# Split weights in rings: eight tiles of 512 columns, or four of 1024

## The chip, the cores and the metric

The kernel runs on one core of one Trainium2 chip. The metric is the device time of one execution in microseconds (us), lower is better. TensorE (PE) multiplies, VectorE (DVE) and ScalarE (ACT) work element by element, GpSimd (POOL) does the same for a few small steps, and SyncE (SP) issues the transfers. Each engine runs its own instructions in the order in which they stand in its queue.

## The reference

Two layers (DEPTH 2) run over one sequence of 512 tokens with 1024 features, all in float32. In each layer the normalised input is multiplied by w_in, three groups of heads mix the tokens (differential attention, latent attention, windowed attention), and their outputs are joined by w_out. A cross-attention into 256 memory tokens follows, then a gated feed-forward of width 2816. Each of the three adds its normalised result to the stream.

```python
for l in range(DEPTH):
    h = rmsnorm(x, g_mix_pre[l])
    # three groups of heads from h @ w_in[l]: o_a, o_b, o_c
    mix = jnp.concatenate([o_a, o_b, o_c], axis=-1) @ w_out[l]
    x = x + rmsnorm(mix, g_mix_post[l])
    xo = cross_attention(rmsnorm(x, g_x_pre[l]), rmsnorm(mem, g_x_mem[l]), w_xq[l], w_xkv[l], w_xo[l])
    x = x + rmsnorm(xo, g_x_post[l])
    gate, up = jnp.split(rmsnorm(x, g_ffn_pre[l]) @ w_ffn_in[l], 2, axis=-1)
    x = x + rmsnorm((jax.nn.silu(gate) * up) @ w_ffn_out[l], g_ffn_post[l])
```

## The kernel before

**A product in three.** Every float32 operand of a large product is kept as a high part and a low part, both in the type float32r. `split` makes them: ScalarE casts the source to the high tile (L103), and VectorE subtracts that from the source to get the low tile (L104). `mm3` then issues three matmuls for each block of 128 rows: high by high (L150), and two that take one low part (L151 and L152). Which of the two takes the low weight depends on the side on which the weights stand.

**The rings.** Weights come in by `stage`, which issues the loads of one block of up to 8 x 256 columns into one of two buffers st. `unit` cuts such a block into tiles and splits each: the high tile is named wh, the low tile wl, and both come from the pool w (bufs=8 before), so that each name has a ring of eight buffers of 512 columns. A new tile waits until the matmuls of the tile that had its buffer are through. A unit whose product is a chunk of 128 output features by all tokens (`ws_chunk`) is 8 blocks of 128 columns, so two tiles before; a unit of rows of 512 columns is one tile for each row block. The last down weights of each feed-forward (`down_weights(NG - 1, True)`) also live in this ring, as four pieces of 512 columns; the other down weights have buffers of their own (dwh, dwl) and are split by operations of 1024 columns.

**The stages.** In each layer the mixing runs first (scores, softmax and values of the heads, with the projections filled in between), then the output projection (`out_late`, `out_rest`), then cross-attention (`x_attn`), its output projection, and the feed-forward (`ffn`). Between stages the four token tiles i = 0 to 3 are normalised one after the other: the post-norm squares (L202, ScalarE, one for each half), takes a root on GpSimd (L206, L207: rpost), multiplies by the gain (L236) and adds to x (L238); the pre-norm squares x, takes a root (rpre) and scales (L223 on VectorE, or L220 and L221), and `to_T` transposes the result on PE (L183) and splits it into the high and low tiles of the next stage (hx in cross-attention, hf in the feed-forward, hT in the next layer). The first products of the next stage are made for token tiles 0 and 1 first, and for 2 and 3 when these are there.

**The feed-forward.** Each of 11 groups has four units (gate and up, for two chunks), 4 x 24 matmuls, and then the eight down blocks of the group before (six matmuls each, PSUM tile ps_sc, two buffers), which VectorE adds to the accumulators (L1250; the first group is copied on ScalarE, L1248). The activation is L1233 (ScalarE) and L1234 (VectorE), and its product is split into f.

**What sets the order.** The program names the operations in the order of its code, and a scheduler then places them into the queues of the engines by priorities, dependencies and its own estimates; it does so anew when the operations change. `Head` of the next layer makes the latent projection of the next mixing while the last blocks of the feed-forward run.

## Time and profile before

| | us |
|---|---|
| median of 3 runs | 1578.89 |
| lowest and highest | 1577.57 and 1579.68 |
| the profiled execution's own time | 1577.31 |
| span of the profiled execution | 1575.5 |
| PE busy | 1538.4 |
| DVE busy | 982.5 |
| ACT busy | 804.8 |

The profile shows one execution. Its span runs from the first to the last instruction; its own time is 1.8 us longer. In rows of the time line the first number is the start, the second the duration of one instruction or of a run of equal ones (xcount), and what stands in brackets is how long the engine had been idle and what ended that.

### The profile page before, as it was taken

What the parts mean: (1) busy time and instruction counts of PE and PEld (TensorE: products, weight loads), DVE (VectorE), ACT (ScalarE), POOL (GpSimd) and SP (SyncE); (2) the same over time, 40 slices, a digit from 0 to 9 for tenths busy, and PEclk for the clock granted to TensorE, in tenths of its full rate; (3) what the DMA queues carried; (4) which work ended last, traced back from release to release, by engine and by line L of the source; (5) the groups of instructions that cost most, each with busy time, mean ns of one, the idle gap of its engine ahead of it and who ended that gap; (6) DMA issues with size and microseconds to landing.
All of it is one profiled execution on the core that took longest, in us unless ns stands there. A gap on an engine that the chain in (4) does not pass through costs nothing.

```text
span 1575.5 us, 21925 instructions
## 1 busy us (share of the span) xinstructions
PE 1538.4 (98%) x8225; PEld 1309.8 (83%) x8225; DVE 982.5 (62%) x1919; ACT 804.8 (51%) x1749; POOL 110.3 (7%) x204
## 2 busy tenths in 40 slices
PE   6999999999999999999999999999999999999998
PEld 6987987899888888888888878778888888888886
DVE  6899886765653444454566998858646444445544
ACT  4588888544643232222456788975445532322321
POOL 2200000200300000000130000002004000000000
PEclk9999999999999999999999999999999999999999
DMA  5542651241243222232335144522402423233221
GB/s 179 158 97 88 207 170 41 71 161 54 81 134 113 101 90 98 84 120 91 96 120 146 51 138 164 167 62 86 155 31 97 134 81 107 80 108 107 80 81 54
DMA packets 130298, 168.68 MB, mean 107 GB/s; under 512 B 21776, under 2 KB 100752, under 8 KB 129424
## 3 DMA queue, kind: packets, MB, share of 16 engines
q1 hardware_dynamic: 130192, 167.28, 33.1%
q8 instruction: 65, 1.06, 0.3%
q14 instruction: 41, 0.34, 0.1%
HBM read 150.88 MB, written 10.09 MB: 102 GB/s over the span
## 4 chain that ended last, share of the span: by engine, by line
PE 86%; DVE 5%; ACT 3%; POOL 3%; issue 2%; DMA 1%; SPq 0%; POOLq 0%; DVEq 0%; ACTq 0%
PE ps_mm L152 14%; PE ps_mm L151 13%; PE ps_mm L150 13%; PE ps_av L151 6%; PE ps_av L152 6%; PE ps_av L150 6%; PE ps_sc L152 5%; PE ps_sc L151 5%; PE ps_sc L150 5%; PE ps_at L416 3%; PE ps_sc L801 1%; PE ps_av L589 1%; PE ps_av L590 1%; PE ps_sc L638 1%; DVE x L238 1%
## 5 line engine op out<-in xcount | busy, mean ns | idle before, releaser
L104 DVE TENSOR_TENSOR wl<-st,wh 128x512 fp32r<-128x512 f32 (+1 forms) x406 | 275.5, 691 | 239.9 <-ACT wh L103 239.1
L103 ACT CAST wh<-st 128x512 fp32r<-128x512 f32 (+1 forms) x406 | 243.0, 616 | 294.1 <-PE ps_mm L151 125.0
L151 PE MATMUL ps_mm<-hfl,wh 128*128 128x512 f32 (+1 forms) x384 | 143.0, 372 | 1.5 <-DVE hfl L104 1.5
L152 PE MATMUL ps_av<-hfh,wl 128*128 128x512 f32 (+1 forms) x384 | 142.8, 372 | 1.3 <-DVE wl L104 1.3
L152 PE MATMUL ps_mm<-hfh,wl 128*128 128x512 f32 (+1 forms) x384 | 142.7, 372 | 1.1 <-DVE wl L104 1.1
L150 PE MATMUL ps_mm<-hfh,wh 128*128 128x512 f32 (+1 forms) x384 | 142.7, 372 | 0.6 <-ACT hfh L103 0.6
L150 PE MATMUL ps_av<-hfh,wh 128*128 128x512 f32 (+1 forms) x384 | 142.6, 372 | 0.0
L151 PE MATMUL ps_av<-hfl,wh 128*128 128x512 f32 (+1 forms) x384 | 142.6, 371 | 0.0
L150 PE MATMUL ps_sc<-dwh,f 128*128 128x512 f32 x320 | 124.7, 390 | 0.0
L151 PE MATMUL ps_sc<-dwl,f 128*128 128x512 f32 x320 | 124.5, 389 | 0.0
L152 PE MATMUL ps_sc<-dwh,f 128*128 128x512 f32 x320 | 124.5, 389 | 0.0
L103 ACT CAST dwh<-st 128x1024 fp32r<-128x1024 f32 x40 | 40.1, 1049 | 157.4 <-PE ps_sc L152 153.3
L104 DVE TENSOR_TENSOR pl<-ps_at,ph 128x512 fp32r<-128x512 f32 (+1 forms) x128 | 82.7, 654 | 22.2 <-ACT ph L103 21.0
L206 POOL TENSOR_SCALAR rpost<-rpostss 128x1 f32<-128x1 f32 x24 | 10.5, 436 | 1171.7 <-ACT hTh L202 703.4
L151 PEld LDWEIGHTS ps_mm<-hfl,wh 128*128 128x128 f32 x384 | 72.3, 188 | 15.0 <-DVE hfl L104 2.6
L152 PEld LDWEIGHTS ps_av<-hfh,wl 128*128 128x128 f32 x384 | 72.2, 188 | 14.1 <-DVE wl L104 1.7
L152 PEld LDWEIGHTS ps_mm<-hfh,wl 128*128 128x128 f32 x384 | 72.4, 189 | 13.8 <-DVE wl L104 1.3
L150 PEld LDWEIGHTS ps_mm<-hfh,wh 128*128 128x128 f32 x384 | 72.2, 188 | 13.5 <-ACT hfh L103 1.1
L150 PEld LDWEIGHTS ps_av<-hfh,wh 128*128 128x128 f32 x384 | 72.4, 188 | 12.5
L151 PEld LDWEIGHTS ps_av<-hfl,wh 128*128 128x128 f32 x384 | 72.3, 188 | 12.4
L103 ACT CAST ph<-ps_at 128x512 fp32r<-128x512 f32 (+1 forms) x128 | 70.4, 562 | 23.6 <-PE ps_at L416 22.7
L416 PE MATMUL ps_at<-ident,e 128*128 128x128 f32 x480 | 77.0, 275 | 3.8 <-DVE memTl L104 2.1
(363 smaller groups left out, 3867.2 us busy)
## 6 DMA issues: line engine op xcount, KB each, us to landing
st<-in_w_ffn_in SPq DMA_DIRECT2D x44, 1024.0 KB, 4.9
st<-in_w_ffn_out SPq DMA_DIRECT2D x22, 1024.0 KB, 4.8
st<-in_w_xkv SPq DMA_DIRECT2D x16, 1024.0 KB, 5.3
st<-in_w_out SPq DMA_DIRECT2D x16, 512.0 KB, 4.9
st<-in_w_xq SPq DMA_DIRECT2D x8, 1024.0 KB, 5.1
st<-in_w_xo SPq DMA_DIRECT2D x8, 1024.0 KB, 5.0
st<-in_w_in SPq DMA_DIRECT2D x12, 512.0 KB, 3.9
q<-stg SPq DMA_DIRECT2D x48, 128.0 KB, 2.3
```

The lines of the kernel that those rows point to most:

```text
L103: cast = nc.scalar.copy(hi, src)
L104: nc.vector.tensor_tensor(out=lo, in0=src, in1=hi.bitcast(F32), op=ALU.subtract)
L150: nc.tensor.matmul(ps, lhsT=lh, rhs=rh, start=first, stop=False)
L151: nc.tensor.matmul(ps, lhsT=lh, rhs=rl, start=False, stop=False)
L152: nc.tensor.matmul(ps, lhsT=ll, rhs=rh, start=False, stop=last)
L206: nc.gpsimd.tensor_scalar(out=r, in0=ms[:, 0:1], scalar1=ms[:, 1:2], scalar2=EPS, op0=ALU.add, op1=ALU.add)
L238: nc.vector.scalar_tensor_tensor(out=xt[i][:, sl], in0=t, scalar=r, in1=xt[i][:, sl], op0=ALU.mult, op1=ALU.add)
L416: nc.tensor.transpose(pt[:, c * P:(c + 1) * P], e[:, k * P:(k + 1) * P], ident)
L589: nc.tensor.matmul(av, lhsT=v, rhs=hi, start=k == u["k0"], stop=False)
L590: nc.tensor.matmul(av, lhsT=v, rhs=lo, start=False, stop=k == u["k1"] - 1)
L638: nc.tensor.matmul(ps, lhsT=t[:, m, 0, i * P:(i + 1) * P], rhs=t[:, m, 1, :], start=True, stop=True)
L801: nc.tensor.matmul(ps, lhsT=mla["qT"][:, h, i * P:(i + 1) * P], rhs=mla["kT"][:, h, :], start=True, stop=True)
```

## The change

The pool of the ring has four buffers instead of eight, and a tile holds up to 1024 columns instead of 512. A unit of 8 x 128 columns is then one tile, split by one cast and one subtraction of twice the width; a unit of four rows of 512 columns is two tiles. The memory of the rings stays the same. A piece of 512 columns takes a whole buffer all the same, so the last down weights fill four buffers of four, where they filled four of eight. No matmul is added or taken away.

```diff
-    wp = ctx.enter_context(tc.tile_pool(name="w", bufs=8))
+    wp = ctx.enter_context(tc.tile_pool(name="w", bufs=4))
...
         a, b = st_view.shape[1], st_view.shape[2]
-        per = 512 // b
+        per = 1024 // b
```

Since the instructions changed, the scheduler's order did too. Three places are shown. Names carry buffer numbers where rows would read alike.

In a steady group of the feed-forward, VectorE's queue at the end of the fourth unit (e is the gated product, f its split, faccM the accumulator) stood like this before:

```order
L1234 TENSOR_TENSOR e<-e,ps_av 128x512
L104 TENSOR_TENSOR wl<-st,wh 128x512
L1250 TENSOR_TENSOR faccM<-faccM,ps_sc 128x512
L104 TENSOR_TENSOR f_6284<-e,f_6284 128x512
L1250 TENSOR_TENSOR faccM<-faccM,ps_sc 128x512 x3
L1250 TENSOR_TENSOR faccSq<-faccSq,ps_sc 128x512 x4
```

and stands like this now:

```order
L1234 TENSOR_TENSOR e<-e,ps_av 128x512
L104 TENSOR_TENSOR wl<-st,wh 128x1024
L104 TENSOR_TENSOR f_5369<-e,f_5369 128x512
L1250 TENSOR_TENSOR faccM<-faccM,ps_sc 128x512 x4
L1250 TENSOR_TENSOR faccSq<-faccSq,ps_sc 128x512 x4
```

The last low split is the wide one, and f stands ahead of the first accumulation instead of behind it.

On PE at the same place, the down blocks (ps_sc, six matmuls each) and the first unit of the next group (ps_mm) before, from the third block on:

```order
L150 MATMUL ps_sc_6899<-dwh_6877,f0_6505 128x512
L151 MATMUL ps_sc_6899<-dwl_6878,f0_6505 128x512
L152 MATMUL ps_sc_6899<-dwh_6877,f0_6505 128x512
L150 MATMUL ps_sc_6899<-dwh_6877,f0_6505 128x512
L151 MATMUL ps_sc_6899<-dwl_6878,f0_6505 128x512
L152 MATMUL ps_sc_6899<-dwh_6877,f0_6505 128x512
```

and now, from the end of the second block on:

```order
L150 MATMUL ps_sc_6543<-dwh_6529,f0_6189 128x512
L151 MATMUL ps_sc_6543<-dwl_6530,f0_6189 128x512
L152 MATMUL ps_sc_6543<-dwh_6529,f0_6189 128x512
L150 MATMUL ps_mm_6612<-hfh0_4533,wh_6604 128x512
L151 MATMUL ps_mm_6612<-hfl0_4534,wh_6604 128x512
L152 MATMUL ps_mm_6612<-hfh0_4533,wl_6605 128x512
L150 MATMUL ps_mm_6612<-hfh0_4533,wh_6604 128x512
L150 MATMUL ps_sc_6551<-dwh_6529,f0_6189 128x512
L151 MATMUL ps_sc_6551<-dwl_6530,f0_6189 128x512
L152 MATMUL ps_sc_6551<-dwh_6529,f0_6189 128x512
```

Four matmuls of the next group's first unit stand between the second and the third block; before they came behind the eighth.

At the start of cross-attention, VectorE's queue around the normalisation of token tile 3 (x3, scaled into the tiles c), with the low tiles of units 1 to 3 and the transposed tiles hxl, before (the low tiles of unit 1 had come earlier):

```order
L236 TENSOR_TENSOR e_3893<-ps_av_3605,gains_3685 128x512
L238 SCALAR_TENSOR_TENSOR x3_3695<-e_3892,rpost_3889,x3_3695 128x512
L238 SCALAR_TENSOR_TENSOR x3_3695<-e_3893,rpost_3889,x3_3695 128x512
L104 TENSOR_TENSOR wl_3923<-st_3920,wh_3922 128x512
L104 TENSOR_TENSOR wl_3927<-st_3920,wh_3926 128x512
L223 SCALAR_TENSOR_TENSOR c_3904<-x3_3695,rpre_3901,gains_3685 128x512
L104 TENSOR_TENSOR hxl0_3689<-ps_at_3966,hxh0_3688 128x4x128
L104 TENSOR_TENSOR hxl1_3691<-ps_at_3973,hxh1_3690 128x4x128
L223 SCALAR_TENSOR_TENSOR c_3905<-x3_3695,rpre_3901,gains_3685 128x512
L104 TENSOR_TENSOR wl_3931<-st_3920,wh_3930 128x512
L104 TENSOR_TENSOR wl_3935<-st_3920,wh_3934 128x512
```

and now:

```order
L236 TENSOR_TENSOR e_3733<-ps_av_3445,gains_3525 128x512
L238 SCALAR_TENSOR_TENSOR x3_3535<-e_3732,rpost_3729,x3_3535 128x512
L238 SCALAR_TENSOR_TENSOR x3_3535<-e_3733,rpost_3729,x3_3535 128x512
L104 TENSOR_TENSOR wl_3753<-st_3412,wh_3752 128x1024
L104 TENSOR_TENSOR hxl0_3529<-ps_at_3794,hxh0_3528 128x4x128
L104 TENSOR_TENSOR hxl1_3531<-ps_at_3801,hxh1_3530 128x4x128
L223 SCALAR_TENSOR_TENSOR c_3744<-x3_3535,rpre_3741,gains_3525 128x512
L223 SCALAR_TENSOR_TENSOR c_3745<-x3_3535,rpre_3741,gains_3525 128x512
L104 TENSOR_TENSOR wl_3759<-st_3756,wh_3758 128x1024
L104 TENSOR_TENSOR wl_3763<-st_3756,wh_3762 128x1024
```

The low tile of unit 1 stands behind the residual of tile 3 (L238), and those of units 2 and 3 behind both scalings of c. On PE the products of unit 1 (ps_av) followed the transposes of o before:

```order
L183 MATMUL ps_at_3973<-ident_95,o_3845 128x128 x4
L150 MATMUL ps_av_3939<-hxh0_3688,wh_3912 128x256
L151 MATMUL ps_av_3939<-hxl0_3689,wh_3912 128x256
L152 MATMUL ps_av_3939<-hxh0_3688,wl_3913 128x256
L150 MATMUL ps_av_3939<-hxh0_3688,wh_3912 128x256
L151 MATMUL ps_av_3939<-hxl0_3689,wh_3912 128x256
L152 MATMUL ps_av_3939<-hxh0_3688,wl_3913 128x256
```

and now units 2 and 3 begin ahead of the first product with a low tile:

```order
L183 MATMUL ps_at_3801<-ident_95,o_3685 128x128 x4
L150 MATMUL ps_av_3767<-hxh0_3528,wh_3752 128x256
L151 MATMUL ps_av_3767<-hxl0_3529,wh_3752 128x256
L150 MATMUL ps_mm_3768<-hxh0_3528,wh_3758 128x256
L151 MATMUL ps_mm_3768<-hxl0_3529,wh_3758 128x256
L150 MATMUL ps_av_3769<-hxh0_3528,wh_3762 128x256
L151 MATMUL ps_av_3769<-hxl0_3529,wh_3762 128x256
L152 MATMUL ps_av_3767<-hxh0_3528,wl_3753 128x256
L150 MATMUL ps_av_3767<-hxh0_3528,wh_3752 128x256
```

Two matmuls each of units 1, 2 and 3 stand ahead of the L152 that reads the low tile.

At the start of the feed-forward in layer 1, VectorE's queue around the normalisation of token tiles 2 and 3 (scaled into o and c), with the transposed tiles hfl and the low tiles of units 0 to 3, before:

```order
L223 SCALAR_TENSOR_TENSOR o_5050<-x2_3694,rpre_5054,gains_4718 128x512
L104 TENSOR_TENSOR wl_5141<-st_5130,wh_5140 128x512
L104 TENSOR_TENSOR wl_5145<-st_5130,wh_5144 128x512
L236 TENSOR_TENSOR e_5106<-ps_mm_5060,gains_4718 128x512
L238 SCALAR_TENSOR_TENSOR x3_3695<-e_5105,rpost_5102,x3_3695 128x512
L238 SCALAR_TENSOR_TENSOR x3_3695<-e_5106,rpost_5102,x3_3695 128x512
L104 TENSOR_TENSOR wl_5213<-st_5128,wh_5212 128x512
L104 TENSOR_TENSOR wl_5217<-st_5128,wh_5216 128x512
L223 SCALAR_TENSOR_TENSOR c_5112<-x3_3695,rpre_5116,gains_4718 128x512
L104 TENSOR_TENSOR hfl0_4722<-ps_at_5174,hfh0_4721 128x4x128
L104 TENSOR_TENSOR hfl1_4724<-ps_at_5181,hfh1_4723 128x4x128
L104 TENSOR_TENSOR wl_5221<-st_5130,wh_5220 128x512
```

and now:

```order
L223 SCALAR_TENSOR_TENSOR o_4830<-x2_3534,rpre_4834,gains_4530 128x512
L104 TENSOR_TENSOR wl_4917<-st_4910,wh_4916 128x1024
L104 TENSOR_TENSOR wl_4985<-st_4908,wh_4984 128x1024
L236 TENSOR_TENSOR e_4886<-ps_mm_4840,gains_4530 128x512
L238 SCALAR_TENSOR_TENSOR x3_3535<-e_4885,rpost_4882,x3_3535 128x512
L238 SCALAR_TENSOR_TENSOR x3_3535<-e_4886,rpost_4882,x3_3535 128x512
L104 TENSOR_TENSOR hfl0_4534<-ps_at_4946,hfh0_4533 128x4x128
L104 TENSOR_TENSOR hfl1_4536<-ps_at_4953,hfh1_4535 128x4x128
L104 TENSOR_TENSOR wl_4989<-st_4910,wh_4988 128x1024
L223 SCALAR_TENSOR_TENSOR c_4892<-x3_3535,rpre_4896,gains_4530 128x512
```

The split of unit 2 moved ahead of the residual of tile 3 (L238), and that of unit 3 ahead of the scaling of c (L223).

## Rows read from the trace of the kernel before

**Rows 1.** Busy times and shares of all engines, the page's first part.

```profile
PE 1538.4 (98%) x8225; PEld 1309.8 (83%) x8225; DVE 982.5 (62%) x1919; ACT 804.8 (51%) x1749; POOL 110.3 (7%) x204
```

**Rows 2.** Windows: length, busy time (instructions) per engine, PEclk, DMA share, GB/s.

```profile
80.00:120.00 40.00, 39.89 (x214) 33.44 (x213) 38.68 (x97) 32.21 (x72) 0.00 (x0) 1.00 0.38 92
...
480.00:740.00 260.00, 260.00 (x1148) 215.35 (x1148) 121.88 (x170) 77.13 (x118) 0.00 (x0) 1.00 0.29 96
```

**Rows 3.** Windows of tile wl alone: PE, PEld, DVE.

```profile
80.00:120.00 40.00, 14.70 (x38) 6.96 (x37) 6.73 (x10) 1.00 0.38 92
```

**Rows 4.** Groups by form: busy, mean ns of one, idle before.

```profile
L104 DVE TENSOR_TENSOR wl<-st,wh 128x512 fp32r<-128x512 f32 x386 | 264.4, 697 | 238.7 <-ACT wh L103 238.0
...
L104 DVE TENSOR_TENSOR dwl<-st,dwh 128x1024 fp32r<-128x1024 f32 x40 | 47.2, 1222 | 32.7 <-ACT dwh L103 32.7
...
L103 ACT CAST wh<-st 128x512 fp32r<-128x512 f32 x386 | 232.5, 620 | 288.5 <-PE ps_mm L151 120.4 <-PE ps_av L151 103.0 <-DMA st<-in_w_ffn_in 37.4
...
L103 ACT CAST dwh<-st 128x1024 fp32r<-128x1024 f32 x40 | 40.1, 1049 | 157.4 <-PE ps_sc L152 153.3 <-DMA st<-in_w_ffn_out 4.1
```

**Rows 5.** Time line of DVE: start, us, equal operations in a run.

```profile
280.61 2.50 DVE L104 TENSOR_TENSOR wl<-st,wh 128x512 fp32r<-128x512 f32 x4 [0.54 <-ACT wh L103]
...
520.58 2.36 DVE L104 TENSOR_TENSOR dwl<-st,dwh 128x1024 fp32r<-128x1024 f32 x2 [0.44 <-ACT dwh L103]
```

**Rows 6.** Time lines of PE, DVE and ACT, one group of the feed-forward.

```profile
541.01 0.39 PE L150 MATMUL ps_sc<-dwh,f 128*128 128x512 f32 x1
...
543.73 0.39 PE L150 MATMUL ps_sc<-dwh,f 128*128 128x512 f32 x1
...
542.57 0.69 DVE L1250 TENSOR_TENSOR faccM<-faccM,ps_sc 128x512 f32<-128x512 f32 x1
...
541.04 0.62 ACT L103 CAST wh<-st 128x512 fp32r<-128x512 f32 x1 [2.10 <-PE ps_av L151]
```

**Rows 7.** Time lines of PE and ACT, start of the feed-forward in both layers.

```profile
438.01 0.39 PE L152 MATMUL ps_av<-hfh,wl 128*128 128x256 f32 x1 [0.49 <-DVE wl L104]
...
1210.98 0.39 PE L152 MATMUL ps_mm<-hfh,wl 128*128 128x256 f32 x1 [1.14 <-DVE wl L104]
...
1214.89 0.39 PE L152 MATMUL ps_av<-hfh,wl 128*128 128x256 f32 x1 [0.79 <-DVE wl L104]
...
428.08 1.12 ACT L103 CAST wh<-st 128x512 fp32r<-128x512 f32 x2
```

**Rows 8.** Time lines of PE, DVE and ACT, start of cross-attention, layer 1.

```profile
309.44 1.04 PE L183 MATMUL ps_at<-ident,o 128*128 128x128 f32 x8
...
320.27 0.39 PE L151 MATMUL ps_mm<-hxl,q 128*128 128x256 f32 x1 [0.17 <-DVE hxl L104]
...
309.94 1.40 DVE L238 SCALAR_TENSOR_TENSOR x<-e,rpost,x 128x512 f32<-128x512 f32 x2
...
311.27 1.28 DVE L104 TENSOR_TENSOR wl<-st,wh 128x512 fp32r<-128x512 f32 x2
...
313.39 0.75 DVE L223 SCALAR_TENSOR_TENSOR c<-x,rpre,gains 128x512 f32<-128x512 f32 x1 [0.85 <-POOL rpre L207]
...
312.07 1.05 ACT L103 CAST hxh<-ps_at 128x512 fp32r<-128x512 f32 x2
```

**Rows 9.** Time lines of PE, ACT and DVE, start of layer 2.

```profile
790.54 0.36 PE L150 MATMUL ps_av<-wh,hTh 128*128 128x256 f32 x1
...
797.72 1.16 PE L183 MATMUL ps_at<-ident,o 128*128 128x128 f32 x8 [1.31 <-DVE hTl L104]
...
809.47 1.09 PE L183 MATMUL ps_at<-ident,c 128*128 128x128 f32 x8 [1.08 <-ACT c L221]
...
791.07 0.60 ACT L103 CAST wh<-st 128x512 fp32r<-128x512 f32 x1
...
793.57 0.68 DVE L1250 TENSOR_TENSOR faccSq<-faccSq,ps_sc 128x512 f32<-128x512 f32 x1
```

**Rows 10.** Time line of SP, the store of the distances.

```profile
54.07 0.53 SPq L334 DMA_DIRECT2D dist_dram<-dist  x1
```

## The prediction

> **What bounds the kernel now.** I read the page's busy times first [rows 1]: TensorE (PE) is busy for 1538.4 of 1575.5 us, so all of its idle time is 37 us, and a change that adds or removes no matmul moves the time only through those 37 us and through new waits. The second view is the table by windows [rows 2]: in the feed-forward stretch PE is never idle while VectorE (DVE) is busy for 121.88 of 260 us; in the mixing stretch DVE is busy for 38.68 of 40 us and PE for 39.89. So DVE has room everywhere except in mixing. The third view is the groups by form [rows 4], which price a split; the last are the rows around the places where the order of the work moves [rows 6 to 10]. PE waits for a low tile (wl) three times in all, for 0.49, 1.14 and 0.79 us [rows 7]. That is everything a cheaper split could give back directly.
>
> **What the change removes.** 193 pairs of splits of 512 columns become 193 of 1024 (386 of the old form on each engine [rows 4]; the 416s and 384s go the same way). Mean durations say 2 x 0.697 - 1.222 = 0.172 us saved on DVE for each pair. Back to back it is less: four low splits take 2.50 us, so they start (2.50 - 0.69) / 3 = 0.603 us apart, and two of 1024 start 2.36 - 1.22 = 1.14 us apart [rows 5]; a pair saves 2 x 0.603 - 1.14 = 0.066 us. A queue that runs dry saves nothing. Only mixing has a full DVE queue: ten low splits lie in its first window [rows 3], so about 40 in its four windows (two in each layer), an estimate; 20 pairs x 0.066 = 1.3 us of DVE time. PE is idle for only 0.11 us in that window, so I take half: **-0.6 us**. Bounds: -3.4 (20 x 0.172, one for one on PE) to +2, since the order there is shuffled and a long split can stand ahead of a softmax step; each layer could then gain a wait like the longest of rows 7, about 1 us.
>
> **What it delays.** A ring tile is whole only when both its operations are: the first half was ready after 0.620 + 0.697 = 1.32 us, the whole after 1.049 + 1.222 = 2.27 us [rows 4], 0.95 us later. PE's third matmul of a unit needs the low tile. Whether that shows depends on place.
>
> *Feed-forward, steady.* The new order puts the last wide split and the cast residue f ahead of the first accumulation, and moves four matmuls of the next group up between down blocks 2 and 3. ScalarE's cast starts when PE lets go of the slot, 541.04 [rows 6], and ends at 542.09; the wide DVE split runs from there, f follows 1.14 later (543.26), the first accumulation 0.60 later (543.86), done at 544.55 by the 0.69 of its row. Block 3 needs that PSUM buffer. It started at 543.73; twelve matmuls lie between 541.01 and 543.73, 0.227 each, so four more make 544.64. The cover is 0.09, less the signal between the engines, for which I allow 0.05 to 0.15: a wait of 0 to 0.06 us, in 8 groups of each layer that accumulate on DVE: 16 x 0.03 = **+0.5 us**. Bounds 0 and 16 x 0.15 = 2.4, the latter if the operations follow at full durations (542.09 + 1.22 + 0.69 + 0.69 = 544.69, plus 0.1). Everything else in these stretches is made one group ahead and hidden by its 32 us of matmuls; slot releases, and so SyncE's loads, move by under 1 us.
>
> *Feed-forward, start.* The split of unit 2 now stands ahead of token tile 3's residual, and that of unit 3 ahead of its scaling into c, which waits for GpSimd. In layer 1 ScalarE casts unit 1 from 428.08 [rows 7]; its low tile is done 1.05 + 1.22 later (430.4), unit 2's at 431.5, and unit 3's, behind two residual steps and two transposed tiles, at 435.8 to 436.8. PE wants it at 437.5: the 0.49 goes. In layer 2 the 1.14 and 0.79 go, but unit 1, which PE reaches sooner after its first wait than in layer 1, has by my estimate half of its 0.95 us uncovered, which adds 0.5, and unit 3 may wait for 0.2. Sum -0.5 - 1.93 + 0.7 = **-1.8 us** (-2.6 to -0.8).
>
> *Cross-attention, start.* Here three low splits moved the other way, behind the residual of token tile 3. PE transposes tile 2 from 309.44 for 1.04 us [rows 8], of which about 0.2 overlaps what follows, then runs two matmuls of each of three units (256 columns, half of 0.227, 0.12 each) and wants unit 1's low tile at 311.05. DVE begins the residual at 309.94 because it waits for a root on GpSimd, and the next operation at 311.27. That slot now holds the wide split: ready at 312.49, a wait of 1.4 us that was not there, as both halves of this tile used to be split ahead of the residual. 22 matmuls later PE is at 315.3 and transposes c. ScalarE now squares the second half of tile 3 behind two casts (1.05 us [rows 8]), so c starts at 314.35 instead of 313.39 and its two halves end at 315.7: 0.1 us. Unit 2's low tile follows, 315.65 + 1.22 = 316.87, against 316.2: 0.7 us. Unit 3's is ready at 318.0 and needed at 319.5. The old wait of 0.17 goes. Sum 1.4 + 0.1 + 0.7 - 0.17 = 2.0, and layer 2 has the same order there: **+4.0 us** (+1, if the residual comes earlier as less stands before it, to +5). DVE is idle for 0.85 us just before c while PE will wait.
>
> The Trainium skill, page "Perfetto Trace Analysis", section "Optimizing Scalar/DVE Operations", says that larger operations help where the engine is saturated, and that where it is not but makes bubbles on other engines, breaking instructions up may let work finish sooner. Rows 2 and 8 are one case of each.
>
> *Start of layer 2.* The last down weights still take a whole slot for each 512 columns; they filled four of eight slots and now fill all four. The two tiles of the next layer's latent projection therefore wait for the last blocks of layer 1. Their first cast takes the place at 791.07 [rows 9] and is done at 792.1, where PE wanted it at 790.54; six matmuls moved up, then the low tile behind the accumulation at 793.57: 794.2 + 1.22 = 795.4, against 793.8. PE reaches the transposes at 799.6 instead of 797.72, where it already waited for 1.31. The chain of token tile 3 that ends at 809.47 does not start later, and PE waits there for 1.08, so most of the 1.9 is absorbed: **+0.7 us** (0 to +3).
>
> *The rest.* Program start and last blocks: the same waits for loads and normalisations end last; 0 (within 0.5). PE keeps its matmuls, GpSimd its work, and SyncE its transfers: on its queue the store of the distances passes twelve copies of q, 0.53 us to issue [rows 10]; its data are ready on DVE ahead of the tile that those copies wait for, and they feed mixing some 20 us later, so 0.
>
> **How the numbers follow.** -0.6 + 0.5 - 1.8 + 4.0 + 0.7 = +2.8, against the profiled execution: 1577.31 (span 1575.5) becomes 1580.1. That execution lies 1.58 below the median of the runs, 1578.89, so the same sum from the median gives 1581.7, rounded to **1581.5 us**. A measurement of this kernel can tell about 0.2% (3.2 us) from no change; the forecast lies just inside that.
>
> **Rivals.**
> 1. *The change hides altogether* (chance 0.16): the residual in cross-attention moves up by what no longer stands before it, and the wait falls to the lower bound: -0.6 - 1.8 + 1 + 0.5 = -0.9, 1578.0 us. For it: 98% busy PE and mostly idle DVE. Against: the residual waits for GpSimd, not for DVE's queue.
> 2. *Slower: the cover of block 3 fails* (0.24). It decides once the first accumulation ends more than 0.1 us past 544.64, since that comes 16 times: 0.15 each gives +2.4 for the 0.5, so 1581.5 + 1.9 = 1583.4, the middle of this case 1585; wholly without the four matmuls 0.9 each, 1581 + 14.4 = 1595. For it: 0.09 of cover. Against: all its durations are rows with little spread. The upper bound at the start of layer 2 gives 1584.
> 3. *Faster: mixing is bound by DVE at full durations* (0.14). Then -3.4 there, and with the lower bounds elsewhere (+1, -2.6, 0, 0) -5.0: 1573.9. For it: 38.68 of 40 us busy. Against: the 0.603 spacing, and PE's 39.89. The Trainium skill, page "VectorE: DVE Perf Modes", section "The DRAIN you can't avoid", has the next operation wait until the pipe is empty, which would give the 0.172; rows 5 do not agree, and the page itself excepts operations that are not held.
>
> The forecast has 0.46; 0.24 of it lies within 0.2%, 0.22 beyond, since its sum ends near the bound. Within: 0.24 + 0.16 = 0.40. Slower: 0.22 + 0.24 = 0.46. Faster: 0.14. The range runs from 1575.5, leaving out most of rival 3, to 1588, leaving out only the failed cover at more than a third of its size.
>
> **What would show it.** Right: PE waits of about 1.4 and 0.7 us for wl near 311 and 316 and 776 us later; none near 438, 1211 and 1215; feed-forward PE at 100%; wide splits 1.14 apart. Wrong: waits of PE for an accumulation in every feed-forward group; no new wait in cross-attention; a mixing stretch shorter or longer by over 2 us.

## The result, and the profile after

| | before | after |
|---|---|---|
| median (us) | 1579.29 | 1587.16 |
| lowest and highest | 1577.57 and 1580.97 | 1586.62 and 1587.95 |
| span of the profiled execution | 1575.5 | 1585.6 |

The ratio is 1.0054, with an interval of 1.0043 to 1.0066: the changed kernel is slower by 7.9 us, and its fastest run is longer than the slowest run of the kernel before. The forecast of 1581.5 was on the right side and 5.7 us too low; the time lies just inside the range.

The page of the changed kernel first: the busy times, and the two groups of the split (line, engine, operation, tiles and shapes, count, then busy time, mean ns of one, idle time ahead and its releasers).

```profile
PE 1542.8 (97%) x8225; PEld 1309.0 (83%) x8225; DVE 960.2 (61%) x1721; ACT 772.6 (49%) x1551; POOL 111.9 (7%) x204
...
L103 ACT CAST wh<-st 128x1024 fp32r<-128x1024 f32 (+3 forms) x208 | 211.0, 1020 | 325.4 <-PE ps_av L151 147.6
L104 DVE TENSOR_TENSOR wl<-st,wh 128x1024 fp32r<-128x1024 f32 (+3 forms) x208 | 247.5, 1194 | 192.1 <-ACT wh L103 187.6
```

Against [rows 1] DVE does 22.3 us less work and ACT 32.2 less, in 198 instructions fewer on each. The edit did what it says, and what it saved lay beside other work. PE is busy for 4.4 us more with the same 8225 matmuls: a part of what the change cost lies inside matmuls and is no idle time. The rest shows in PE's waits (releaser, us in total, times, longest), here of the changed kernel, the start of the program and the four groups that name the ring's tiles:

```profile
PE ps_at L183 <- DVE o L223: 11.1, 3, 10.1
PE ps_av L152 <- DVE wl L104: 3.3, 2, 1.6
...
PE ps_av L151 <- DVE wl L104: 2.0, 1, 2.0
...
PE ps_mm L152 <- DVE wl L104: 1.8, 3, 1.0
...
PE ps_av L150 <- ACT wh L103: 1.4, 1, 1.4
```

Of the first row, 10.1 us are the start of the program. The ring's tiles have 3.3 + 2.0 + 1.8 + 1.4 = 8.5 us, where PE before waited for wl three times, 2.42 us in all [rows 7].

The rest of this document goes by stages. The boundaries are starts of PE's instructions in the time line, in the kernel before: the first instruction (10.56), the first cross-attention product (306.57), the first transposes towards the feed-forward (416.11), its first and its tenth down group (475.73, 769.49), the transpose of the first tile of the second latent projection (831.61), then 1082.88, 1192.39, 1252.62, 1546.38 and the last matmul (1567.95). The first line gives the length of each stage before, the others what is added to it. All are single profiled executions.

| kernel | mixing 1 | cross-att. 1 | ff start 1 | ff 1 | start of layer 2 | mixing 2 | cross-att. 2 | ff start 2 | ff 2 | end |
|---|---|---|---|---|---|---|---|---|---|---|
| before | 296.01 | 109.54 | 59.62 | 293.76 | 62.12 | 251.27 | 109.52 | 60.22 | 293.76 | 21.58 |
| after | +3.72 | +2.45 | -0.84 | +0.83 | +1.63 | +0.58 | +2.39 | -1.43 | +0.81 | -0.01 |
| e_narrow | +1.69 | +0.61 | +0.43 | +0.73 | +4.96 | +2.23 | +0.63 | -0.17 | +0.73 | -0.01 |
| e_x | +3.64 | +2.08 | -0.85 | +0.75 | +1.64 | +0.98 | +2.07 | -1.44 | +1.07 | +0.03 |
| e_ring | +2.77 | +2.46 | -0.84 | +0.81 | +0.01 | +0.66 | +2.37 | -1.45 | +0.89 | 0.00 |
| e_u3 | +3.68 | +2.47 | -1.24 | +1.19 | +1.62 | +0.72 | +2.37 | -1.41 | +1.19 | -0.01 |
| e_mix | +0.26 | +1.78 | -1.25 | +0.76 | +3.13 | +3.40 | +1.75 | -1.86 | +0.76 | -0.01 |
| f_late | +2.30 | +2.49 | -1.25 | +0.21 | +1.60 | +0.70 | +2.38 | -1.87 | +0.12 | -0.01 |
| f_x1 | +3.60 | +1.38 | -1.25 | +0.75 | +1.63 | +1.15 | +1.41 | -1.43 | +0.75 | -0.01 |
| b_h0 | +1.31 | +0.01 | -0.77 | 0.00 | -0.04 | +3.19 | -0.02 | -1.36 | 0.00 | 0.00 |
| c_nar | +1.83 | +0.81 | -0.81 | +0.20 | -0.17 | +1.94 | +0.83 | -1.42 | +0.20 | 0.00 |
| c_pri | +2.41 | +1.23 | -0.81 | +0.21 | -0.19 | +1.56 | +1.58 | -1.81 | +0.17 | 0.00 |

How far may such a difference be trusted? In mixing b_h0 has the same order as the kernel before, and its two mixing stages are 1.31 and 3.19 us longer all the same. In the first, a cast waits for a load of w_xkv that SyncE issued at the same place (at 129.32 us, before at 129.08); the first row is ScalarE in b_h0, the second in the kernel before:

```profile
136.83 0.62 ACT L103 CAST wh<-st 128x512 fp32r<-128x512 f32 x1 [1.38 <-DMA st<-in_w_xkv]
...
135.21 0.62 ACT L103 CAST wh<-st 128x512 fp32r<-128x512 f32 x1
```

In the other stages kernels with the same code agree within 0.1 to 0.5, but for the start of layer 2 in e_mix. So mixing is uncertain by 1 to 3 us in each execution (by such a load, and by the clock of the last section), and the rest is not. It also tells why the line after sums to 10.1 where the medians differ by 7.9: in both layers the profiled execution of before has the shortest mixing of all twelve.

The places of the prediction in the changed kernel, as PE's time line has them (start, us, in brackets the idle time and what ended it): cross-attention and start of the feed-forward in both layers, and the start of layer 2.

```profile
316.21 0.39 PE L152 MATMUL ps_av<-hxh,wl 128*128 128x256 f32 x1 [1.63 <-DVE wl L104]
320.42 0.39 PE L152 MATMUL ps_mm<-hxh,wl 128*128 128x256 f32 x1 [0.42 <-DVE wl L104]
...
433.27 0.39 PE L151 MATMUL ps_mm<-hfl,wh 128*128 128x256 f32 x1 [1.23 <-DVE hfl L104]
...
797.85 0.39 PE L150 MATMUL ps_av<-wh,hTh 128*128 128x256 f32 x1 [1.36 <-ACT wh L103]
801.62 0.39 PE L151 MATMUL ps_av<-wl,hTh 128*128 128x256 f32 x1 [2.01 <-DVE wl L104]
814.10 0.39 PE L152 MATMUL ps_mm<-hTh,wl 128*128 128x256 f32 x1 [0.97 <-DVE wl L104]
...
1097.20 0.38 PE L152 MATMUL ps_av<-hxh,wl 128*128 128x256 f32 x1 [1.63 <-DVE wl L104]
1101.41 0.39 PE L152 MATMUL ps_mm<-hxh,wl 128*128 128x256 f32 x1 [0.41 <-DVE wl L104]
...
1214.15 0.39 PE L151 MATMUL ps_mm<-hfl,wh 128*128 128x256 f32 x1 [1.24 <-DVE hfl L104]
```

The new waits in cross-attention are there, twice in each layer; the three waits of [rows 7] are gone; at the start of layer 2 three waits for the ring stand in place of the two of [rows 9].

### The profile page after: what moved, and what is told of

It reads as the page before. It is cut to its first block, busy times and chain, and to the rows that moved or that the text cites. A ratio compares the mean times of both kernels' runs of the same rounds, so it can differ in the third digit from the quotient of the medians.

```text
span 1585.6 us, 21396 instructions
## 1 busy us (share of the span) xinstructions
PE 1542.8 (97%) x8225; PEld 1309.0 (83%) x8225; DVE 960.2 (61%) x1721; ACT 772.6 (49%) x1551; POOL 111.9 (7%) x204
## 5 line engine op out<-in xcount | busy, mean ns | idle before, releaser
L103 ACT CAST wh<-st 128x1024 fp32r<-128x1024 f32 (+3 forms) x208 | 211.0, 1020 | 325.4 <-PE ps_av L151 147.6
L104 DVE TENSOR_TENSOR wl<-st,wh 128x1024 fp32r<-128x1024 f32 (+3 forms) x208 | 247.5, 1194 | 192.1 <-ACT wh L103 187.6
L152 PE MATMUL ps_mm<-hfh,wl 128*128 128x512 f32 (+1 forms) x384 | 142.6, 371 | 0.0
L152 PE MATMUL ps_av<-hfh,wl 128*128 128x512 f32 (+1 forms) x384 | 142.6, 371 | 0.0
L152 PE MATMUL ps_sc<-dwh,f 128*128 128x512 f32 x320 | 124.6, 389 | 0.0
L1234 DVE TENSOR_TENSOR e<-e,ps_av 128x512 f32<-128x512 f32 x44 | 30.3, 688 | 137.8 <-PE ps_av L152 136.5
L152 PEld LDWEIGHTS ps_mm<-hfh,wl 128*128 128x128 f32 x384 | 72.3, 188 | 12.6
L152 PEld LDWEIGHTS ps_av<-hfh,wl 128*128 128x128 f32 x384 | 72.3, 188 | 12.5
```

The lines of the kernel that those rows point to most:

```text
L103: cast = nc.scalar.copy(hi, src)
L104: nc.vector.tensor_tensor(out=lo, in0=src, in1=hi.bitcast(F32), op=ALU.subtract)
L152: nc.tensor.matmul(ps, lhsT=ll, rhs=rh, start=False, stop=last)
L1234: nc.vector.tensor_tensor(out=fv, in0=sg, in1=pss[2 * c + 1], op=ALU.mult)
```

## The experiments

The edits below are against the changed kernel, but for b_h0, which is against the kernel before. Where a tile is to be split by two operations of half its width, the helper is this:

```python
cuts = lambda hi, lo, src, n, cut: [split(hi[:, j:j + h], lo[:, j:j + h], src[:, j:j + h])
                                    for h in [max(1, n // 2) if cut else n] for j in range(0, n, h)]
```

**e_narrow: narrow operations in the new buffers.** Every tile of 1024 is split by two operations of 512.

```diff
-            split(hi, lo, st_view[:, k0:k1, :])
+            cuts(hi, lo, st_view[:, k0:k1, :], k1 - k0, True)
```

> The four buffers of 1024 columns stay, but each tile is split by two casts and two subtractions of 512 columns (416 and 384 likewise) instead of one of each. Theory W (the long operation, and where it stands in VectorE's queue, makes the new waits): cross-attention gives its 2.45 us per layer back, mixing its 3.26 and 0.56, the steady feed-forward its 0.10 per group; the gain of 0.85 and 1.43 at the start of the feed-forward is lost; the 1.63 at the start of layer 2 stays, since the ring is full there all the same. Sum against the changed kernel: -4.9 - 3.8 - 1.65 + 2.3 = -8.1 us, that is before + 1.6. Theory G (the coarse buffer, freed as a whole, makes them): the waits stay and the time is that of the changed kernel, before + 8 to 9.

Measured: 1588.5 us, ratio 1.0054 (1.0039 to 1.0069). As a total theory W has failed: it asked for 8.1 us less than the changed kernel, and nothing came back. By the stages cross-attention gives back 1.8 us in each layer and the first mixing 2.0, but the gain at the start of the feed-forward is lost (+0.43, -0.17), and the second mixing (+2.23) and the start of layer 2 (+4.96) are longer than in the changed kernel. So the gain at the start of the feed-forward is not the buffers'. At the start of layer 2 PE waits 0.95 us more than in the changed kernel, and most of the rest is the clock, shown in the last section; all four runs are long, and whether the clock fell in the other three no trace shows.

Feed-forward is no faster (+0.73), but that does not clear the width. The first accumulation does end sooner, 3.29 us after the first down product of a group instead of 3.54. The scheduler put three matmuls of the next group ahead of the third block instead of four, and with them went 0.227 us of cover.

**e_x: narrow only in cross-attention.** The three first ring units there.

```diff
-        us = [first[0], unit(first[1][:, :, P:2 * P])]
+        us = [first[0], unit(first[1][:, :, P:2 * P], True)]
...
-        us += [unit(st[:, :, 0:P]), unit(st[:, :, P:2 * P])]
+        us += [unit(st[:, :, 0:P], True), unit(st[:, :, P:2 * P], True)]
```

> The changed kernel, with the three ring units at the start of cross-attention alone split by two narrow operations each. If the waits of 1.63 and 0.42 us for the low tiles come from the wide split behind the residual of token tile 3: they go in both layers, and the span falls by 4.9 us against the changed kernel (1587.2 to 1582.3), nothing else moves. If the late scaling of tile 3 on ScalarE and GpSimd is what ends the stage: the low-tile waits go but the transposes of c wait instead, and 1 us at most per layer comes back.

Measured: 1588.68 us, 1.0059 (1.0044 to 1.0074). Cross-attention is +2.08 instead of +2.45: 0.4 of 2.4 comes back, as the second alternative had it, and the median shows nothing of it. The waits for wl shrank to 0.85 and 0.10, but the scaling into o is late then, and PE waits 0.31 for that.

**e_ring: the last down weights in whole buffers.**

```diff
-                return [(Halves(a), Halves(b)) for a, b in
-                        (zip(*(unit(st[:, c:c + 1, 512 * h:512 * (h + 1)])[0] for h in range(2))) for c in range(2))]
+                return (unit(st[:, 0:1, :]) + unit(st[:, 1:2, :]))
```

> The changed kernel, with the last down weights as two ring tiles of 1024 columns instead of four pieces of 512, so that two of four buffers stay free for the latent projection of layer 2. If the full ring makes the waits of 1.36 and 2.01 us there: the cast and split of that projection come some 20 us earlier, both waits go, and the 1.63 us of the boundary fall to 0 or a little below (1587.2 to 1585.5). If the chain of token tile 3 sets the end there: no change beyond 0.5 us.

Measured: 1584.89 us, 1.0036 (1.0024 to 1.0048). The start of layer 2 goes from +1.63 to +0.01, and PE's waits between 788 and 822 us become these:

```profile
PE ps_at L927 <- DVE hTl L104: 1.4, 1, 1.4
PE ps_at L183 <- ACT o L221: 0.6, 1, 0.6
PE ps_mm L152 <- DVE wl L104: 0.2, 1, 0.2
```

The ring's 1.36 + 2.01 + 0.97 are gone, and what is left has the size of before [rows 9]. The loss at this place was four buffers taken by four pieces of half their size.

**e_u3: narrow for the last unit of a feed-forward group.** The up unit of the second chunk, from group 1 on; the expectation speaks of both units of that chunk, the edit has the last alone.

```diff
-                us += [..., unit(stu[:, :, P * c:P * (c + 1)])]
+                us += [..., unit(stu[:, :, P * c:P * (c + 1)], g > 0 and c == 1)]
```

> The changed kernel, with the units of the second chunk in feed-forward groups 1 to 10 split by two narrow operations. The 0.10 us that each steady group lost is put down to the first accumulation ending too late behind the wide split. The first narrow subtraction can start when half of the cast is done, so the accumulation ends about 0.23 us earlier and the 0.10 goes: -1.6 us (1587.2 to 1585.6), down blocks 32.64 us apart again. If instead the four matmuls moved up cost it, by their own start behind the blocks: 32.74 stays.

Measured: 1588.98 us, 1.0067 (1.0048 to 1.0086). Feed-forward is +1.19 in each layer, longer than with the wide split. In one group the first down product, the third block and the first accumulations stand so:

```profile
546.56 0.39 PE L150 MATMUL ps_sc<-dwh,f 128*128 128x512 f32 x1
...
549.98 0.50 PE L150 MATMUL ps_sc<-dwh,f 128*128 128x512 f32 x1
...
549.24 1.27 DVE L1250 TENSOR_TENSOR faccM<-faccM,ps_sc 128x512 f32<-128x512 f32 x2
```

The first of the two accumulations ends 3.36 us after that product, 0.18 sooner than the 3.54 of the changed kernel, as expected. But here too three matmuls of the next group stand ahead of the third block instead of four, 0.227 less, and PE waits longer. So neither this run nor e_narrow parts the width from the order. f_late moves the split away from there.

**e_mix: narrow only in mixing,** in both layers, with the first latent projection.

```diff
-    head = Head(0, hT)
+    state["narrow"] = True; head = Head(0, hT)
...
-        mixT = mix_phase(l, head)
+        state["narrow"] = True; mixT = mix_phase(l, head); state["narrow"] = False
```

> The changed kernel, with four buffers of 1024 columns as it has them, but in the mixing stage of both layers (and the first latent projection) each tile is split by two operations of 512 columns again. Theory W, the width of the operations makes mixing slower (a long split stands ahead of a short step of a softmax or of the scaling of a transposed tile): by the first cross-attention products of layer 1 the changed kernel was 3.7 us behind the kernel before, counted from PE's first instruction; here it is 1.7, as in e_narrow, and mixing of layer 2, 0.56 behind, is level. That is 2.0 to 2.5 us less than the changed kernel: 1584.7 to 1585.2. Theory R, the coarser release of the four buffers does it (a cast waits until both halves of a buffer are read): nothing comes back in mixing, 3.7 and 0.56 stay, 1587.2. Both leave cross-attention, feed-forward and the start of layer 2 as in the changed kernel.

Measured: 1585.88 us, 1.0039 (1.0025 to 1.0053). Mixing of layer 1 is +0.26 instead of +3.72. That is more than the theory of the width asked for, and the uncertainty of mixing is in it; mixing of layer 2 is +3.40, with a stretch at the lower clock. Cross-attention, expected as in the changed kernel, is +1.78 and +1.75. Against their own runs of the kernel before, the medians are +5.8 here and +7.9 for the changed kernel. A mark that comes early is sharper: the score product (L638) that starts 59.32 us after PE's first instruction before. In the six executions with wide splits in mixing (after, e_x, e_ring, e_u3, f_late, f_x1) it starts 1.00 to 1.10 us later, in b_h0 0.07 earlier, and in the four with narrow splits in buffers of 1024 (e_narrow, e_mix, c_nar, c_pri) 0.42 to 0.56 earlier. So the width costs 1.5 us by there, and the coarser buffers cost nothing. The four are still 0.37 to 0.54 ahead at the last score product of layer 1, 115 us after PE's first instruction: up to there theory R has fallen. Two waits of PE show where the width acts, the first two rows from the changed kernel and the third from the kernel before, which has only that one:

```profile
44.64 0.43 PE L150 MATMUL ps_mm<-wh,hTh 128*128 128x416 f32 x1 [0.59 <-DVE stg L466]
63.99 0.30 PE L927 MATMUL ps_at<-ident,m 128*128 128x128 f32 x1 [0.74 <-DVE m L922]
...
63.40 0.30 PE L927 MATMUL ps_at<-ident,m 128*128 128x128 f32 x1 [0.30 <-DVE m L922]
```

In e_mix, that stretch (36 to 116.6 us) has neither. 0.59 and the 0.44 more for m make 1.03 of the 1.05 us. ScalarE and DVE of the changed kernel explain the first:

```profile
41.56 0.68 ACT L465 ACTIVATE stg<-ps_mm,dscale 128x512 fp32r<-128x512 f32 x1
...
42.82 1.02 DVE L104 TENSOR_TENSOR wl<-st,wh 128x832 fp32r<-128x832 f32 x1
43.75 0.74 DVE L466 SCALAR_TENSOR_TENSOR stg<-ps_mm,dscale,stg 128x512 fp32r<-128x512 f32 x1
```

PE waits for L466 to empty its PSUM buffer and starts at 44.64, 0.15 us after the 44.49 at which L466 ends. What L466 subtracts was ready on ACT when L465 ended, 41.56 + 0.68 = 42.24; L466 stood behind the wide split until 43.75.

The other wait is not one of DVE's queue: DVE is idle for 0.77 us ahead of L922 and waits for a root on GpSimd, in either kernel. What grew is GpSimd's first step of that root, L156, which runs beside the split. Changed kernel, then the kernel before:

```profile
61.50 1.23 DVE L104 TENSOR_TENSOR wl<-st,wh 128x1024 fp32r<-128x1024 f32 x1 [0.52 <-ACT wh L103]
61.91 0.90 POOL L156 TENSOR_SCALAR lr<-lms 128x1 f32<-128x1 f32 x1 [4.58 <-ACT m L920]
...
60.84 1.29 DVE L104 TENSOR_TENSOR wl<-st,wh 128x512 fp32r<-128x512 f32 x2
61.77 0.44 POOL L156 TENSOR_SCALAR lr<-lms 128x1 f32<-128x1 f32 x1 [4.67 <-ACT m L920]
```

The step takes 0.22 us where no operation of DVE runs beside it. Here it ends 0.08 us after the split in both kernels (62.81 and 62.73, before 62.21 and 62.13), and the wide split ends later.

**f_late: the last split behind the first accumulation.**

```diff
-                us += [unit(stg_[:, :, P * c:P * (c + 1)]), unit(stu[:, :, P * c:P * (c + 1)])]
+                us += [unit(stg_[:, :, P * c:P * (c + 1)])]
+                with tc.issue_after(state["sum"]) if c and state["sum"] else nullcontext():
+                    us += [unit(stu[:, :, P * c:P * (c + 1)])]
...
-                nc.vector.tensor_tensor(out=accv(i, h), in0=accv(i, h), in1=ps, op=ALU.add)
+                a_ = nc.vector.tensor_tensor(out=accv(i, h), in0=accv(i, h), in1=ps, op=ALU.add)
+                if i == h == 0: state["sum"] = a_.ins
```

> The changed kernel, but in feed-forward the split of a group's last unit is held back until the first accumulation of the blocks that run beside it has been issued (the data it makes are wanted by PE some 25 us later). VectorE's order there is then: product, accumulation, f, wide split, accumulations, where the changed kernel has product, wide split, f, accumulations. Theory Q (the 0.10 us that each group got longer is PE's third block waiting for its PSUM buffer, whose accumulation stands behind the wide split): the groups come 32.64 us apart again instead of 32.74 in the eight groups of each layer that accumulate on VectorE, 1.6 us in all, 1585.6. Theory R (the group is longer since the ring of four is released later): 32.74 stay, 1587.2.

Measured: 1586.19 us, 1.0042 (1.0027 to 1.0058). Feed-forward is +0.21 and +0.12 instead of +0.83 and +0.81. First DVE and PE of the changed kernel, then DVE of f_late, at the end of one group's products:

```profile
546.28 0.69 DVE L1234 TENSOR_TENSOR e<-e,ps_av 128x512 f32<-128x512 f32 x1 [3.38 <-PE ps_av L152]
547.12 1.23 DVE L104 TENSOR_TENSOR wl<-st,wh 128x1024 fp32r<-128x1024 f32 x1 [0.15 <-ACT wh L103]
548.26 0.69 DVE L104 TENSOR_TENSOR f<-e,f 128x512 fp32r<-128x512 f32 x1
548.86 1.28 DVE L1250 TENSOR_TENSOR faccM<-faccM,ps_sc 128x512 f32<-128x512 f32 x2
...
549.63 0.47 PE L150 MATMUL ps_sc<-dwh,f 128*128 128x512 f32 x1
549.94 0.39 PE L151 MATMUL ps_sc<-dwl,f 128*128 128x512 f32 x1
```

```profile
512.04 0.69 DVE L1236 TENSOR_TENSOR e<-e,ps_av 128x512 f32<-128x512 f32 x1 [3.38 <-PE ps_av L152]
513.33 0.69 DVE L1252 TENSOR_TENSOR faccM<-faccM,ps_sc 128x512 f32<-128x512 f32 x1 [0.60 <-PE ps_sc L152]
513.93 0.68 DVE L104 TENSOR_TENSOR f<-e,f 128x512 fp32r<-128x512 f32 x1
514.54 1.22 DVE L104 TENSOR_TENSOR wl<-st,wh 128x1024 fp32r<-128x1024 f32 x1
```

In the changed kernel the first accumulation ends at 548.86 + 0.69 = 549.55; PE's next block, the third, starts at 549.63, and its first matmul takes 0.31 to the next instead of 0.227. That 0.08, hidden in a matmul and called no wait by the view, is most of the 0.10 by which a group grew (32.74 from one to the next instead of 32.64). In f_late the accumulation, L1252 there, ends 514.02 - 511.77 = 2.25 us after the group's first down product, against 549.55 - 546.01 = 3.54, and PE does not wait. The four matmuls of the next group stand behind the third block again, so the run undid the place on DVE and on PE together. The split that now comes later is wanted only by the last products of the next group.

**f_x1: the wide split of cross-attention's first unit ahead.**

```diff
-        us = [first[0], unit(first[1][:, :, P:2 * P])]
+        with tc.high_priority(offset=HASTE): us = [first[0], unit(first[1][:, :, P:2 * P])]
```

> The changed kernel, but at the start of cross-attention the split of the first ring unit has priority: on VectorE it stands ahead of token tile 2's second sum and residual instead of behind token tile 3's residual. Theory P (the place of that one wide split costs the 2.4 us of each layer): PE's waits for wl of 1.63 and 0.42 us go and nothing takes their place, 1582.4. Theory C (VectorE's chain of residual, square, root and scaling of token tiles 2 and 3 ends the stage as soon as the splits don't): the chain starts up to 1.14 us later behind the split, the waits for wl turn into waits for o or c of the same size, and the stage is between 0.5 us shorter and 1 us longer in each layer, 1586.2 to 1589.2. After e_x I hold C for likelier.

Measured: 1586.07 us, 1.0044 (1.0028 to 1.0059). PE in f_x1:

```profile
314.88 0.63 PE L183 MATMUL ps_at<-ident,o 128*128 128x128 f32 x4 [1.14 <-DVE o L223]
...
319.25 0.38 PE L152 MATMUL ps_mm<-hxh,wl 128*128 128x256 f32 x1 [0.19 <-DVE wl L104]
```

The wait of 1.63 for wl is now a wait of 1.14 for o: counted from the first product of the stage, DVE begins to scale o 3.52 us in (313.99 - 310.47), against 1.84 (311.67 - 309.83) in the changed kernel. The chain of residual, square, root and scaling pays for the place that the split got. Theory C, as held likelier, though a little better than its numbers: +1.4 a layer, 1.0 less than the changed kernel. Narrow operations there and in the weights ahead of them (e_narrow, c_nar) come to +0.6 to +0.8: a short operation may fit into the pieces in which DVE waits for GpSimd, which no run here tests.

**b_h0: the kernel before, with another order at the start of the feed-forward.**

```diff
-                us += [unit(stg_[:, :, P * c:P * (c + 1)]), unit(stu[:, :, P * c:P * (c + 1)])]
+                with tc.high_priority(offset=HASTE) if g == 0 else nullcontext():
+                    us += [unit(stg_[:, :, P * c:P * (c + 1)]), unit(stu[:, :, P * c:P * (c + 1)])]
```

> The kernel before with its eight buffers of 512 columns; only the splits of feed-forward's first group have priority, so that on VectorE and ScalarE they stand ahead of the sums, the residual and the scaling of token tile 3, without any change in width. Theory O (what the changed kernel gains at the start of feed-forward, 0.85 and 1.43 us, is the order, not the width): PE's waits for wl of 0.49, 1.14 and 0.79 us there go, and the kernel comes to 1576.9 to 1577.4. Rival: the splits moved up push the chain of token tile 3 back by up to 1.8 us, of which VectorE's idle pieces before it (0.41, 0.36 and 0.77 us) take 1.5; PE then waits for c instead, and the kernel stays at 1579.3 or loses up to 1 us.

Measured: 1577.56 us, 0.9985 (0.9975 to 0.9994): faster than both kernels. The start of the feed-forward is -0.77 and -1.36, as the changed kernel has it (-0.84 and -1.43), with eight buffers and narrow splits. The three waits for wl of [rows 7] are gone, and PE there waits only for transposed tiles (1.30 us in layer 2 too):

```profile
429.17 0.38 PE L151 MATMUL ps_mm<-hfl,wh 128*128 128x256 f32 x1 [1.30 <-DVE hfl L104]
```

So the one gain of the change was its order, and it can be had without the change.

**c_nar and c_pri: the places undone together.** c_nar has e_mix, e_x, e_ring and f_late in one kernel; c_pri has f_x1 in the place of e_x.

> The changed kernel with its places undone together: splits of 512 columns in mixing and for the three first units of cross-attention, the last down weights in two whole buffers (as e_ring), the last unit's split behind the first accumulation (as f_late); four buffers of 1024 and wide splits everywhere else, in feed-forward above all. If the losses are separate and sit where the runs put them, the stages stand against the kernel before as in the runs that undid each: mixing +0.3 to +1.7 in layer 1 and 0 to +0.5 in layer 2 (e_mix, e_narrow), cross-attention +0.6 twice (e_narrow), start of feed-forward -1.25 and -1.85 (f_late), feed-forward +0.2 and +0.1, start of layer 2 0: -0.5 to +1.0 in all, 1579.5 to 1581, no longer told from the kernel before. Rival: the places lean on each other (a split moved out of one queue place lands in the next), and 3 us or more of the 8 remain, 1583 and up.

> As c_nar, but cross-attention's three first units are split wide, with priority for the first of them (as f_x1). f_x1 brought cross-attention from +2.4 to +1.4 in each layer, e_mix from +2.4 to +1.8 since the weights of the output projection ahead of it are split in 512s there; if both add up it is +0.8 a layer, 0.2 above c_nar: 1580 to 1581.5. If VectorE's total work in that stage is what counts, either way of arranging it gives the same, +0.6.

Measured: c_nar 1580.95 us, 1.0005 (0.9996 to 1.0014); c_pri 1580.76 us, 1.0004 (0.9995 to 1.0012). Neither can be told from the kernel before. The losses add up and were where the stages had put them. Within cross-attention c_nar has +0.81 and +0.83 where +0.6 was expected, c_pri +1.23 and +1.58 where +0.8 was: the two ways don't add up there.

## Why the prediction was right, and where it was off

By the stages of one execution each, with the change's own line of the table against the terms of the sum:

- **Mixing, -0.6 forecast: wrong, also in sign.** Measured +3.72 and +0.58; the six wide executions have +2.30 to +3.72 in layer 1, the six narrow ones 0 to +2.41, so about 2 us are the change's there. In layer 2 the wide ones have +0.58 to +1.15 and the narrow ones other than before +1.56 to +3.40: no loss is shown there. The step that failed is "PE is idle for only 0.11 us in that window, so I take half" of what DVE saves. What decided was the sentence put away into the upper bound: a long split can stand ahead of a short step. It did so ahead of L466, and it held up GpSimd's step on which L922 waits.

Two windows show it, mixing in layer 1 before and after (length, busy time of PE, PEld, DVE, ACT and POOL, PEclk, DMA share, GB/s):

```profile
10.56:306.57 296.01, 288.49 (x1681) 245.74 (x1682) 246.85 (x620) 224.44 (x542) 27.49 (x64) 0.99 0.41 123
```

```profile
10.10:309.83 299.73, 290.19 (x1682) 246.81 (x1682) 242.40 (x577) 219.02 (x499) 28.89 (x64) 0.99 0.41 121
```

DVE does 4.45 us less, more than the 1.3 forecast for both layers, and PE is idle for 299.73 - 290.19 = 9.54 us instead of 7.52. The Trainium skill, page "Perfetto Trace Analysis", section "Optimizing Scalar/DVE Operations", says that larger operations can improve throughput where the engine is saturated. [rows 2] have DVE busy for 38.68 of 40 us, and in mixing the wide splits saved DVE's time and lost PE's: the trace agrees for DVE alone, and not for a stage in which others wait for the short steps.

- **Feed-forward, steady, +0.5: right mechanism, too small.** Measured +1.64. The chain was forecast to put the end of the first accumulation at 544.55, and it came at 549.55, which is 544.55 plus the 5.00 by which this group came later. (The forecast's own terms add up to 0.03 less, 542.09 + 1.14 = 543.23 and not 543.26; the wide split starts 0.04 after its cast.) What was off is the allowance for the signal between the engines, behind which no row stood: "0.05 to 0.15" gave 0.03 a group, and it is 0.16, from 549.55 to 549.71, which is 0.227 ahead of the block's second matmul. Less the cover of 0.09 that leaves 0.07, against 0.10 measured, 16 times. It is two thirds of rival 2's smaller price of 2.4, but not by its condition: the accumulation did not end late, the signal was longer.
- **Start of the feed-forward, -1.8: right,** -2.27 measured. (-0.5 - 1.93 + 0.7 is -1.73.) The three waits went, as forecast. The 0.7 us allowed in layer 2 for units 1 and 3 did not come: PE waits for neither, but for hfl, 1.24 us where it waited 0.22.
- **Start of cross-attention, +4.0: right,** +4.84 measured. Forecast were waits of 1.4 and 0.7; they are 1.63 and 0.42. Each costs more than its idle time. The matmul that waited 1.63 starts 1.91 us after the one ahead of it, and the next 0.22 after that, where its neighbours start 0.12 apart: 1.79 + 0.10.
- **Start of layer 2, +0.7: right up to the last step.** +1.63 measured, undone by e_ring. The stage comes 5.70 us later after the change. Less that, the casts start at 791.06 (forecast 791.07) and the low tile's split at 794.16 (794.2); it took 1.70 us instead of 1.22, and PE is at the transposes at 800.19 (799.6). "Most of the 1.9 is absorbed" is what failed, because the chain of token tile 3, said not to start later, did: the residual of token tile 3 starts at 804.69 in that count, 0.93 later than the 803.76 of before, and behind it the next ring tile, with a split of 2.32 us, makes PE wait for 0.97 where it had waited for c.
- **The rest, 0: right.** The last stage is -0.01. The count of 193 pairs is 188 in the trace: ten operations of 512 columns stayed, which changes no term.

The sum of +2.8 became +7.9 by the medians. Of the 5.1 between them feed-forward has 1.1, the start of layer 2 0.9 and cross-attention 0.8, the start of the feed-forward gives 0.5 back, and mixing has the rest, 2.8, a difference of medians and single executions. The forecast was on the right side because the largest term, cross-attention, was right, and the sum was too low because mixing was priced by work instead of by order. That the time lies inside the range, by 0.8 us, is in part luck: the term that brought it to the edge had the wrong sign. Of the prediction's own signs of being wrong two came, a mixing stretch longer by over 2 us (+3.72 in the one execution) and PE held by the accumulation in eight groups of each layer, by 0.1 us each. Rival 1 (all hidden) and rival 3 (a gain in mixing) have fallen.

## What to carry to other kernels

An operation of twice the width costs by what stands behind it in its queue, not by its duration: look for short steps on which another engine waits, and price the place, also in the stage with the fullest queue, and look at the small steps that run beside it on GpSimd. When the size of a buffer grows, look for users that fill only half of one (here the pieces of 512 in a ring of four). When a change of size also changes the order, try the order alone: here it was the whole gain, and the old size kept it. When a run is to part the width from the order, compare the orders first: e_narrow and e_u3 changed both.

## What the runs showed of the hardware that was not expected

TensorE's granted clock falls to its lower level, 1.2 GHz, for a few us, in some executions of the same code and not in others. In e_narrow one lies at the start of layer 2, where PE, at 2.4 GHz until then, was busy for 1.42 of 4.50 us and waited 3.04 us for wl (windows; columns as above):

```profile
793.00:797.50 4.50, 1.42 (x10) 0.85 (x8) 3.36 (x5) 4.19 (x11) 2.25 (x3) 0.93 0.01 5
797.50:801.00 3.50, 2.63 (x12) 2.63 (x13) 3.50 (x6) 1.63 (x5) 1.40 (x3) 0.50 0.36 146
801.00:804.00 3.00, 3.00 (x13) 2.61 (x12) 2.26 (x4) 0.00 (x0) 0.00 (x0) 0.55 0.48 119
```

The changed kernel has 1.00 throughout these windows, though it too waits there, for 2.01 us at the longest. Such stretches lie in three places. In the first mixing seven of the twelve executions have one: the kernel before has 0.57 from 144 to 148 us, the changed kernel 0.66 from 136 to 140, and e_x, e_ring, f_late and f_x1, with the changed kernel's code there, have none; against e_ring the changed kernel falls back by 1.3 us in it. In the second mixing e_narrow, e_mix and b_h0 have one, and at the start of layer 2 e_narrow and e_mix (+3.13, with the changed kernel's code there). So single stages, mixing above all, differ by 1 to 3 us between executions of the same code, by these stretches and by the loads. Only marks ahead of both, or medians of runs, were used against the width.

A split on DVE can be longer while GpSimd multiplies. These are DVE and POOL of the changed kernel:

```profile
799.86 1.70 DVE L104 TENSOR_TENSOR wl<-st,wh 128x1024 fp32r<-128x1024 f32 x1
811.72 2.32 DVE L104 TENSOR_TENSOR wl<-st,wh 128x1024 fp32r<-128x1024 f32 x1
...
798.83 1.65 POOL L220 TENSOR_TENSOR o<-x,gains 128x512 f32<-128x512 f32 x1 [0.93 <-DVE x L238]
811.29 1.67 POOL L220 TENSOR_TENSOR c<-x,gains 128x512 f32<-128x512 f32 x1 [0.47 <-DVE x L238]
```

Overlapped by 0.62 us (799.86 to 800.48) the split took 0.48 more than 1.22, overlapped by 1.24 us (811.72 to 812.96) 1.10 more: nearly the whole overlap is added. It can also go the other way: in the kernel before, at 1200.89, two narrow splits ran beside such a multiplication at their usual 0.68 us each, and the multiplication took 3.48 us instead of 1.68; the root's step in mixing waited likewise. No run here took GpSimd's step away to test it.
